# Head 0's inverse and its pool placed ahead of the closing of the projections' pools; the late gates through two buffers of their own

## The chip, the cores and the metric

The kernel runs on one core of one Trainium2 chip. TensorE (PE) multiplies and transposes, VectorE (DVE), ScalarE (ACT) and GpSimd (POOL) do the elementwise work, and SyncE (SP) issues every DMA from one queue, in order. PE writes its results to PSUM (eight banks); everything else lies in SBUF (224 KB for each of 128 partitions). The metric is the device time of one execution in microseconds; lower is better. All instructions of an engine run in the order in which they stand in its program, so an instruction that waits holds up what stands behind it.

## What is computed

One layer of an encoder trunk on 2048 tokens of width 1024: RMSNorm, one input projection, then two groups of heads, whose outputs meet in one output projection that is added to the residual. The parts that matter here:

```python
h = rms_norm(x, norm_w[l])
proj = h @ w_in[l]
(dn_q, dn_k, dn_v, dn_z, dn_beta, dn_decay,
 sw_q, sw_k, sw_v, sw_z) = jnp.split(proj, cuts, axis=-1)
dn = gated_deltanet_bidir(dn_q, dn_k, dn_v, dn_beta, dn_decay, ...)
dn = rms_norm(dn, dn_out_norm_w[l]).reshape(b, s, DN_WIDTH)
dn = dn * jax.nn.silu(dn_z)
sw = windowed_gqa_with_sinks(sw_q, sw_k, sw_v, ...)
sw = sw * jax.nn.silu(sw_z)
x = x + jnp.concatenate([dn, sw], axis=-1) @ w_out[l]
...
# in gated_delta_rule_chunked, for each head, direction and chunk:
m = jnp.where(strict, jnp.einsum('bhncd,bhnsd->bhncs', k_beta, k) * decay, 0.0)
t_inv = lax.linalg.triangular_solve(eye + m, eye, left_side=True, lower=True, unit_diagonal=True)
```

The DeltaNet group has four heads of width 128. Each head runs a recurrence over the sequence forward and backward, and each chunk of it needs the inverse of a triangular matrix.

## The kernel before

**Stages.** Phase A makes the normalised input, the projections with their gates and convolution, and the windowed attention; its results go to DRAM. Phase B runs the four DeltaNet heads one after another and then the output projection. For head `h`:

- `pre_front(h)` loads keys, queries and values in four groups of four chunks (order 1, 2, 0, 3), transposes them, makes the matrices `ma` and stores them to `m_d`. In each group a power of the keys' squared norms, `nk`, is taken on POOL (L684); `bp`, `ma` and the copy `vs` come after it.
- `solve(h)` loads the 32x32 diagonal blocks of all chunks (`X`, `L`) and inverts them column by column on DVE: 31 pairs of instructions (tiles `tm` and `X`), each pair waiting for the one before. It stores the result to `x_d`.
- `invert(h)` loads `x_d` back in pieces (`xc`), transposes them on DVE (`xt`), copies blocks into the tiles `iv` and `ma` on POOL, and makes the whole inverse with five groups of products on PE (tile `pi`) for each of four pieces (`hi` = 0 to 3).
- `scan(h)` runs 16 steps in both directions at once (tiles `pk`, `py`, `po` on PE; `r`, `S`, `oacc` on DVE; `yk`, `y` on ACT). Its first four steps need only piece 0 of the inverse. `post` normalises and gates the result.

`pre_front(h + 1)`, `solve(h + 1)` and `invert(h + 1)` stand behind `scan(h)` in the text and overlap it on the engines. The output projection's windowed half is cut into 32 units (`sw_units`, tile `pcs`), which fill PE in phase B. The other half (`out_dn`, tile `pcd`, weights `wohd`) ends the program.

**Late gates.** The gates of the second half of the sequence are left out of phase A and run between `pre_front(0)` and `solve(0)` as `late`: four calls of `gate_pairs`, eight output tiles `zo`, PE tile `pf_z`.

**Memory.** Tiles come from pools, which are laid on two stacks, one from each end of SBUF. A pool that opens where older pools lay has to wait for their work; `set_order` plans every use of its tiles behind the last use of all tiles of the older pools that it overlaps. At 128 partitions the places are, in bytes: `xp` 162656 to 228192 (input, split in two), `wp` 123488 to 162656 (weights), `bp` 102848 to 123488 (five buffers of 4128), all three on the right and in the stack `wide`, which is closed after `solve(0)`. On the left `hd0`, `q1` and `qa` (head 0's tiles, `pre_front`'s and `solve`'s) end at 87168. After the closing there open on the right `rp` (the scan's tiles; over `xp`), `hd1` (head 1's tiles; over `wp` and `xp`), `qb` 114912 to 147680 (the inverse's tiles, and two groups of head 2's keys and values; over `bp` and `wp`), and `swp` 88288 to 114912 (the windowed units; over `bp`). The pool `op` of the last projection opens at the end from 55936 to 109184, over `q1`, `qa` and `swp`.

**Order.** The text's order is not the order on the engines. `set_order` builds a graph of all instructions with edges for data, buffers, PSUM banks and pools, plans all engines over it several times with estimated durations, and pins each engine's queue to the best plan. So a change of a pool's place changes edges, and the plan with them, in the whole program.

Of the kernel before, what the change touches and what calls it, by code (L numbers as in the profile page):

```python
# [7 lines left out]
F32 = mybir.dt.float32  # L8
# [59 lines left out]
def phase_a(ctx, wide, tc, t, ident, nw, bd, gp, mix_sw, kq_d, v_d, zdn_d, zsw_d, q_pool):  # L68
# [5 lines left out]
    with tc.using_default_side("right"):  # L74
        xp = wide.enter_context(tc.tile_pool(reuse_waits="tile", name="xp", bufs=2))
        wp = wide.enter_context(tc.tile_pool(reuse_waits="tile", name="wp", bufs=2))
        bp = wide.enter_context(tc.tile_pool(reuse_waits="tile", name="bp", bufs=5))
        pj = wide.enter_context(tc.tile_pool(reuse_waits="tile", name="pj", bufs=3, space=PSUM))
# [127 lines left out]
    def gate_pairs(todo, half, mid=None):  # L206
        ws = [load_w(t["wt"][i // 2], 2 * P, f"z{i}_{half}") for i, _ in todo]
        for nb in range(2):
            for (i, dst), w in zip(todo, ws):
                o = bp.tile([P, 1030], F32, tag="big", name=f"zo{i}_{half}_{nb}")[:, :1024].rearrange("p (j s) -> p j s", j=2)  # L210
                for j in range(2):
                    ps = proj_feat(w, j * P, 2 * half + nb, f"z{i + j}_{half}_{nb}")
                    A.activation(o[:, j], ps, AF.Tanh, scale=0.5)
                    V.scalar_tensor_tensor(o[:, j], o[:, j], 1.0, ps, ALU.add, ALU.mult)
                at = half * 1024 + nb * 512
                for j in range(2):
                    dma(dst[j][:, at : at + 512], o[:, j])
# [169 lines left out]
    for half in range(2):  # L387
# [20 lines left out]
        sw = [lambda i=i: gate_pairs([(16 + i, [zsw_d[i], zsw_d[i + 1]])], half) for i in (0, 2)]  # L408
        conv = [lambda i=i: conv_pair(i, half) for i in (0, 4, 8, 2, 6, 10)]
        if half:  # L410
            fill = conv
            late = sw + [lambda i=i: gate_pairs([(12 + i, zdn_d[i : i + 2])], half) for i in (0, 2)]
# [108 lines left out]
def phase_b(ctx, wide, late, tc, t, ident, consts, hp, mix_dn, mix_sw, kq_d, v_d, zdn_d, zsw_d, dp, out):  # L521
# [97 lines left out]
    qa = pool("qa", stack=pre_stack)  # L619
    ps_i = [pool("ps_i0", stack=pre_stack, space=PSUM), pool("ps_i1", stack=pre_stack, space=PSUM)]  # L620
# [12 lines left out]
    def kv_tile(kind, h, n, name):  # L633
        p, slot = ((0, n), (1, n), (2, n) if n < 2 else (0, n - 2), (0, 2 + n) if n < 2 else (1, n - 2))[h]
        return (hd[p] if p < 2 else qb).tile([P, 4, P], F32, tag=f"{kind}{slot}", name=name, bufs=1)
# [659 lines left out]
```

## Time and profile before

| | us |
|---|---|
| median of three runs | 1291.93 (1291.03 to 1295.85) |
| the profiled execution | 1291.8 |
| its span, first to last instruction | 1290.0 |

| engine | busy, us | share of the span |
|---|---|---|
| PE | 1231.0 | 95% |
| DVE | 903.9 | 70% |
| ACT | 718.4 | 56% |
| POOL | 509.8 | 40% |

The profile's page lists busy time by engine and by groups of instructions; its views cut the same execution into windows, timelines and chains. Times are counted from the first instruction. A matmul's busy time holds its latency, so that matmuls that wait for each other look busier than they are; PE's work is better read from the step between the starts of matmuls that follow each other.

### The profile page before, as it was taken

Reading aid. Unit: us, or ns where it says so; the run is one execution under the profiler, and the core shown is the slowest. Engines: PE = TensorE matmul, PEld = TensorE weight load, DVE = VectorE, ACT = ScalarE, POOL = GpSimd, SP = SyncE. Lnnn points to the kernel's source line nnn. Section 1 sums busy time; section 2 is a strip of 40 time slices with the busy share of each in tenths; the row PEclk is TensorE's granted clock in tenths of the full one; section 3 lists DMA queues with packets and bytes.
Section 4 is the critical chain, followed back from the end, with each engine's and each line's share of the span. In section 5 each row is a group of like instructions: output and inputs, shape, how many; then the busy total and the mean of one; then the engine's idle time right before and its main releaser. Section 6 shows DMA issues by size and latency. Waiting matters only on the chain.

```text
span 1290.0 us, 22619 instructions
## 1 busy us (share of the span) xinstructions
PE 1231.0 (95%) x7162; PEld 1058.8 (82%) x7162; DVE 903.9 (70%) x2266; ACT 718.4 (56%) x2121; POOL 509.8 (40%) x876
## 2 busy tenths in 40 slices
PE   6999989999999999999999997999799899999998
PEld 6998778888889998888888886788688689898876
DVE  4422388999975689999986474689579869656433
ACT  5422254776744577777664325768657845675310
POOL 2230053757612297665320104833582482640000
PEclk9999999999999999999999997999999999999999
DMA  7442243322544433422127736966965875644765
GB/s 260 148 131 84 84 163 121 116 83 90 156 149 145 127 104 103 150 90 75 71 93 234 219 100 204 254 176 200 282 162 174 267 204 172 196 152 133 253 236 207
DMA packets 225511, 205.36 MB, mean 159 GB/s; under 512 B 48496, under 2 KB 175088, under 8 KB 225392
## 3 DMA queue, kind: packets, MB, share of 16 engines
q1 hardware_dynamic: 225392, 203.92, 50.9%
q8 instruction: 57, 0.93, 0.3%
q14 instruction: 62, 0.51, 0.1%
HBM read 138.79 MB, written 65.08 MB: 158 GB/s over the span
## 4 chain that ended last, share of the span: by engine, by line
PE 68%; DVE 13%; issue 6%; DMA 6%; ACT 4%; POOL 3%; SPq 0%; DVEq 0%; POOLq 0%; ACTq 0%
PE pf_c L190 5%; PE pf_c L191 5%; PE pf_c L192 5%; PE pf_z L190 4%; PE pf_z L191 4%; PE pf_z L192 4%; PE pi L772 3%; PE pt L364 3%; DVE acc L241 2%; PE pq_q L201 2%; PE pq_q L202 2%; PE pq_q L203 2%; PE pcd L563 2%; PE pcd L564 2%; PE pcd L562 2%
## 5 line engine op out<-in xcount | busy, mean ns | idle before, releaser
L190 PE MATMUL pf_c<-xhi,wh_c 128*128 128x512 f32 x384 | 151.2, 406 | 3.2 <-DVE acc L241 3.2
L241 DVE SCALAR_TENSOR_TENSOR acc<-pf_c,cw,acc 128x512 f32<-128x512 f32 (+2 forms) x192 | 140.0, 742 | 17.0 <-ACT acc L237 16.1
L191 PE MATMUL pf_c<-xlo,wh_c 128*128 128x512 f32 x384 | 151.0, 404 | 0.0
L192 PE MATMUL pf_c<-xhi,wl_c 128*128 128x512 f32 x384 | 149.8, 404 | 0.0
L359 POOL TENSOR_SCALAR pr<-pr,st 128x384 f32<-128x384 f32 (+1 forms) x128 | 84.8, 679 | 73.2 <-DVE st L357 49.9
L192 PE MATMUL pf_z<-xhi,wl_z 128*128 128x512 f32 x256 | 90.8, 401 | 0.0
L191 PE MATMUL pf_z<-xlo,wh_z 128*128 128x512 f32 x256 | 90.8, 399 | 0.0
L190 PE MATMUL pf_z<-xhi,wh_z 128*128 128x512 f32 x256 | 89.8, 400 | 0.0
L190 PEld LDWEIGHTS pf_c<-xhi,wh_c 128*128 128x128 f32 x384 | 72.7, 190 | 16.9 <-DVE acc L241 3.6
L350 ACT ACTIVATE pr<-pr,st 128x384 f32<-128x384 f32 (+1 forms) x128 | 76.1, 596 | 16.4 <-DVE st L349 14.3
L191 PEld LDWEIGHTS pf_c<-xlo,wh_c 128*128 128x128 f32 x384 | 72.6, 190 | 13.7
L192 PEld LDWEIGHTS pf_c<-xhi,wl_c 128*128 128x128 f32 x384 | 72.4, 189 | 13.8
L368 ACT ACTIVATE ph<-pt 128x512 fp32r<-128x512 f32 x92 | 53.7, 594 | 46.9 <-PE pt L364 41.3
L345 DVE CUSTOM_DVE_ANT_0 pr<-s,mask,sink 128x384 f32<-128x384 f32 (+1 forms) x128 | 72.7, 592 | 4.8 <-PE pt L364 2.5
L364 PE MATMUL pt<-ident,pr 128*128 128x128 f32 x368 | 71.5, 275 | 1.5 <-POOL pr L359 1.4
L826 ACT ACTIVATE yk<-py,ck 128x128 f32<-128x128 f32 x120 | 43.8, 365 | 48.4 <-PE py L821 47.2
L684 POOL TENSOR_TENSOR nk<-ssk,pw 128x4 f32<-128x4 f32 x16 | 16.9, 1059 | 131.0 <-DVE ssk L683 95.0
L703 DVE SCALAR_TENSOR_TENSOR ma<-gh,bp,dc 128x256 f32<-128x256 f32 x128 | 55.0, 476 | 19.4 <-PE gh L694 15.2
L369 DVE TENSOR_TENSOR pl<-pt,ph 128x512 fp32r<-128x512 f32 x92 | 62.0, 683 | 6.9 <-ACT ph L368 6.6
L364 PEld LDWEIGHTS pt<-ident,pr 128*128 128x128 f32 x368 | 48.1, 140 | 16.8 <-POOL pr L359 4.1
L202 PE MATMUL pq_q<-wh_q,xlo 128*128 128x256 f32 x256 | 61.5, 283 | 0.0
L201 PE MATMUL pq_q<-wh_q,xhi 128*128 128x256 f32 x256 | 61.1, 285 | 0.0
(253 smaller groups left out, 3798.4 us busy)
## 6 DMA issues: line engine op xcount, KB each, us to landing
kqc<-kq_d SPq DMA_DIRECT2D x120, 128.0 KB, 2.9
ws_c<-wt SPq DMA_DIRECT2D x48, 256.0 KB, 3.4
xr<-x SPq DMA_DIRECT2D x16, 512.0 KB, 5.3
ws_z<-wt SPq DMA_DIRECT2D x32, 256.0 KB, 3.6
kq<-kq_d SPq DMA_DIRECT2D x16, 512.0 KB, 5.4
m_d<-ma SPq DMA_DIRECT2D x32, 256.0 KB, 5.2
mxs<-mix_sw SPq DMA_DIRECT2D x32, 256.0 KB, 3.6
xrs<-x SPq DMA_DIRECT2D x32, 256.0 KB, 3.5
```

What stands on the lines that cost most here:

```text
L190: T.matmul(ps, hi[:, k, cs], xhi[b][:, k], start=(k == 0), stop=False)
L191: T.matmul(ps, hi[:, k, cs], xlo[b][:, k], start=False, stop=False)
L192: T.matmul(ps, lo[:, k, cs], xhi[b][:, k], start=False, stop=(k == KC - 1))
L201: T.matmul(ps[:, :n], xh, hi[:, k, :n], start=(k == 0), stop=False)
L202: T.matmul(ps[:, :n], xl, hi[:, k, :n], start=False, stop=False)
L241: V.scalar_tensor_tensor(av, ps[:, lo:], cw[:, i, k : k + 1], av, ALU.mult, ALU.add)
L345: V.tensor_tensor_reduce(pr[j][:, :n], ps[:, :n], mask[:, lo * P : hi * P], 1.0, sink[:, hh : hh + 1], ALU.add, ALU.max, accum_out=mx[:, j ...
L350: A.activation(pr[j][:, :n], pr[j][:, :n], AF.Exp, bias=nm[:, j : j + 1], accum_out=den[:, j : j + 1])
L359: G.tensor_scalar(pr[j][:, :n], pr[j][:, :n], den[:, j : j + 1], 1.0, ALU.mult, ALU.mult)
L364: T.transpose(pt[:, j], pr[j][:, (kb - lo) * P : (kb - lo + 1) * P], ident)
L369: V.tensor_tensor(pl, ptf, ph.bitcast(F32), ALU.subtract)
L703: V.scalar_tensor_tensor(ma[d, c4][:, c], gh[:, k], bp[:, d, cc : cc + 1], gms[d][:, c : c + 1].to_broadcast([P, 2, P]), ALU.mult, ALU.mult,)
```

## The change

`bp` is taken off the stack `wide` and closes with phase A. A new pool `qb` for the inverse opens beside `q1` and `qa` on the left, from 87168 to 111744: it lies over `bp` alone. The late gates write into a pool `zp` of two buffers, 115232 to 123488, also over `bp`. `solve(0)`, the six clearings of the `iv` tiles and `invert(0)` stand ahead of `wide.close()`. Head 2's keys and values, which lay in the old `qb`, get a pool `kx` (139488 to 147680, over `wp`), and `swp` moves to 112864 to 139488 (over `bp`, `zp` and `wp`). `op` stays in its place, which now is that of `q1`, `qa` and the new `qb`, and not of `swp`. The arithmetic is unchanged.

```diff
-        bp = wide.enter_context(tc.tile_pool(reuse_waits="tile", name="bp", bufs=5))
+        bp = ctx.enter_context(tc.tile_pool(reuse_waits="tile", name="bp", bufs=5))
...
-    def gate_pairs(todo, half, mid=None):
+    def gate_pairs(todo, half, mid=None, zp=bp):
...
-                o = bp.tile([P, 1030], F32, tag="big", name=f"zo{i}_{half}_{nb}")[:, :1024].rearrange("p (j s) -> p j s", j=2)
+                o = zp.tile([P, 1030], F32, tag="big", name=f"zo{i}_{half}_{nb}")[:, :1024].rearrange("p (j s) -> p j s", j=2)
...
-            late = sw + [lambda i=i: gate_pairs([(12 + i, zdn_d[i : i + 2])], half) for i in (0, 2)]
+            late = sw + [lambda zp, i=i: gate_pairs([(12 + i, zdn_d[i : i + 2])], half, None, zp) for i in (0, 2)]
...
     qa = pool("qa", stack=pre_stack)
+    qb = pool("qb", stack=pre_stack)
...
-        return (hd[p] if p < 2 else qb).tile([P, 4, P], F32, tag=f"{kind}{slot}", name=name, bufs=1)
+        return (hd[p] if p < 2 else kx).tile([P, 4, P], F32, tag=f"{kind}{slot}", name=name, bufs=1)
...
+    with tc.using_default_side("right"):
+        zp = pool("zp", 2, stack=wide)
     H = pre_front(0)
     for f in late:
-        f()
+        f(zp)
     solve(0, H)
+    zts = [[const(f"iv{j}_{i}", [P, 4, P], None, qb) for i in range(2 - j % 2)] for j in range(4)]
+    for grp in zts:
+        for a in grp:
+            G.memset(a, 0.0)
+    invert(0, H)
     wide.close()
     with tc.using_default_side("right"):
         rp = pool("rp", 2)
         hd.append(pool("hd1"))
         ps_s = pool("ps_s", space=PSUM)
-        qb = pool("qb", stack=pre_stack)
+        kx = pool("kx", stack=pre_stack)
         swp = pool("swp", SWW, stack=pre_stack)
-    zts = [[const(f"iv{j}_{i}", [P, 4, P], None, qb) for i in range(2 - j % 2)] for j in range(4)]
-    for grp in zts:
-        for a in grp:
-            G.memset(a, 0.0)
     fill = sw_units(swp)
-    invert(0, H)
```

(The two windowed gates in `sw` get the pool in the same way.) Since the plan decides the order, three places of it are shown. The line numbers of the change are one to three higher than those of before.

**PE, from the last matmul of the projections on.** `pf_z` is a late gate, `tr`, `gh` and `trv` belong to `pre_front(1)`, `pi` to `invert(0)`, `py` to `scan(0)`. Before:

```order
L192 MATMUL pf_z_1_1_8754<-xhi_4485,wl_z_1_8652 128x512
L674 MATMUL tr_1_0_9912<-ident,kq_1_9900 128x128 x4
L694 MATMUL gh_1_0_9944<-kq_1_9900 128x256 x2
L674 MATMUL tr_1_1_9927<-ident,kq_1_9900 128x128 x4
L711 MATMUL trv_1_9968<-ident,vt_1_9902 128x128 x4
L674 MATMUL tr_2_0_9988<-ident,kq_2_9978 128x128 x4
L694 MATMUL gh_1_1_9955<-kq_1_9900 128x256 x2
L674 MATMUL tr_2_1_10003<-ident,kq_2_9978 128x128 x4
L694 MATMUL gh_2_0_10020<-kq_2_9978 128x256
L711 MATMUL trv_2_10044<-ident,vt_2_9980 128x128 x4
```

The first `pi` stands four rows further on, behind the transposes of group 0, and the first `py` 17 rows behind that. With the change:

```order
L192 MATMUL pf_z_1_1_8761<-xhi_4485,wl_z_1_8659 128x512
L675 MATMUL tr_1_0_9919<-ident,kq_1_9907 128x128 x4
L773 MATMUL pi_0_0_8925<-iv_0_8891,g_0_8911 128x128 x4
L695 MATMUL gh_1_0_9951<-kq_1_9907 128x256
L675 MATMUL tr_1_1_9934<-ident,kq_1_9907 128x128 x4
L695 MATMUL gh_1_0_9951<-kq_1_9907 128x256
L773 MATMUL pi_0_0_8940<-b_0_8930,iv_0_8894 128x128 x4
L773 MATMUL pi_0_0_8947<-iv_0_8894,b_0_8930 128x128 x4
L712 MATMUL trv_1_9975<-ident,vt_1_9909 128x128 x4
L773 MATMUL pi_0_0_8956<-iv_0_8896,g_0_8911 128x128 x4
L675 MATMUL tr_2_0_9995<-ident,kq_2_9985 128x128 x4
```

The inverse moved ahead of `pre_front(1)`, and the first `py` stands 17 rows behind the last `pf_z` instead of 30.

**POOL, at the start of `pre_front(1)`** (`nk1` is its power, the other rows clear and fill the inverse's tiles). Before:

```order
L736 MEMSET X0_8784 128x32
L684 TENSOR_TENSOR nk1_9894<-ssk1_9893,pw_4992 128x4
L761 TENSOR_TENSOR g0_0_8923<-ma0_0_8125 128x512
L901 MEMSET iv0_0_8903 128x512
L901 MEMSET iv2_0_8906 128x512
L684 TENSOR_TENSOR nk1_9894<-ssk1_9893,pw_4992 128x4
```

With the change:

```order
L766 COPY iv2_1_8895<-xc0_1_2_8974 32x4x32
L766 COPY iv2_1_8895<-xt0_0_1_8971 32x4x32
L766 COPY iv2_1_8895<-xc0_1_2_8974 32x4x32
L766 COPY iv2_1_8895<-xt0_0_1_8971 32x4x32
L685 TENSOR_TENSOR nk1_9901<-ssk1_9900,pw_4992 128x4
L785 COPY ma0_0_8132<-xc0_1_3_8907 32x4x32
```

The first `nk1` stood first behind the clearing of `X0`; now 27 block copies of the inverse stand between the two, and all clearings of `iv` stand earlier.

**DVE, at the last columns of `solve(2)`** (`tm2`, `X2`), beside `scan(1)` (`r1`, `S1`, `oacc1`; the last number of `oacc1`'s source `po1` before the running one is the step). Before:

```order
L741 TENSOR_TENSOR tm2_30_12113<-L2_12016,X2_12017 128x31
L683 TENSOR_SCALAR ssk3_13095<-ssk3_13095 128x4
L849 SCALAR_TENSOR_TENSOR oacc1_0_10792<-po1_1_15_11437,egc_5026,oacc1_0_10792 128x128
L745 TENSOR_TENSOR X2_12017<-X2_12017,tm2_30_12113 128x31
L703 SCALAR_TENSOR_TENSOR ma3_0_13263<-gh3_0_1_13311,bp3_13097,dc3_0_0_13260 128x2x128
```

With the change:

```order
L742 TENSOR_TENSOR tm2_30_12120<-L2_12023,X2_12024 128x31
L851 TENSOR_TENSOR oacc1_3_10812<-po1_0_12_11263,oacc1_3_10812 128x128
L834 SCALAR_TENSOR_TENSOR S1_1_12_11291<-S1_1_11_11251,egt_5024,po1_1_12_11283 128x128
L746 TENSOR_TENSOR X2_12024<-X2_12024,tm2_30_12120 128x31
L686 RECIPROCAL ssk3_13102<-ssk3_13102 128x4
```

The solve of head 2 ended beside the last step of head 1's scan (15) and now ends beside step 12. For `solve(1)` the order goes the other way: its last three columns stood behind the last `r0` before, and the last seven do now; its first column stood behind `r0` of step 4 and now stands behind that of step 7.

At the end of the program two more things differ: on SP four of the eight loads of `wohd` stand ahead of the store of the last but one windowed unit, where all stood behind the last one's, and on PE the last windowed unit runs between steps 12 and 15 of `scan(3)` instead of beside step 12.

More of the change, by code (lines that the diff above doesn't have):

```diff
@@ L407, in phase_a @@
             consts = delta_setup(tc, t, ident, bd, gp, ap, bp, pj, q_pool)
-        sw = [lambda i=i: gate_pairs([(16 + i, [zsw_d[i], zsw_d[i + 1]])], half) for i in (0, 2)]
+        sw = [lambda zp=bp, i=i: gate_pairs([(16 + i, [zsw_d[i], zsw_d[i + 1]])], half, None, zp) for i in (0, 2)]
         conv = [lambda i=i: conv_pair(i, half) for i in (0, 4, 8, 2, 6, 10)]
```

## The prediction

> **What bounds the kernel now.** I read the page first, then windows, then the timelines where PE stands still. On the page, the row of PE, the 40 slices, and PE's clock:
>
> ```profile
> PE 1231.0 (95%) x7162; PEld 1058.8 (82%) x7162; DVE 903.9 (70%) x2266; ACT 718.4 (56%) x2121; POOL 509.8 (40%) x876
> PE   6999989999999999999999997999799899999998
> PEclk9999999999999999999999997999999999999999
> ```
>
> PE bounds the whole, and the worst slice after the start is the 25th, from 774 to 806 us. That is where the change works: the gates end, head 0's inverse and scan begin. The windows (PE and PEld busy, DVE, ACT, POOL, the granted clock, DMA):
>
> ```profile
> 783.00:817.00 34.00, 25.44 (x126) 19.74 (x124) 19.75 (x47) 24.08 (x106) 20.66 (x42) 0.75 0.90 256
> 850.00:912.00 62.00, 58.79 (x410) 52.56 (x410) 59.64 (x192) 46.22 (x196) 17.17 (x17) 1.00 0.63 192
> 912.00:935.00 23.00, 16.86 (x92) 13.80 (x92) 10.06 (x29) 11.27 (x42) 13.61 (x35) 0.93 0.97 290
> 1018.00:1043.00 25.00, 21.40 (x114) 17.66 (x115) 14.90 (x38) 15.51 (x59) 17.43 (x44) 0.93 0.86 248
> 1130.00:1195.00 65.00, 62.07 (x467) 57.08 (x467) 40.04 (x120) 42.32 (x147) 14.68 (x32) 1.00 0.46 144
> ```
>
> Two things are to be seen. From 783 to 817 PE is neither full nor at full clock. From 850 to 912 DVE is full (59.64 of 62): there `solve(1)` and `scan(0)` share it. At each change of heads PE waits again.
>
> The timelines of 777 to 817 give the chain:
>
> ```profile
> 777.50 0.32 SPq L746 DMA_DIRECT2D x_d<-X  x1
> 785.77 0.57 SPq L217 DMA_DIRECT2D zdn<-zo  x1
> 791.46 0.43 SPq L757 DMA_DIRECT2D xc<-x_d  x1
> 797.71 0.30 DVE L758 STREAM_TRANSPOSE xt<-xc 128x128 f32<-128x128 f32 x1
> 801.58 1.49 PE L772 MATMUL pi<-iv,g 128*128 128x128 f32 x6
> 816.48 0.49 PE L821 MATMUL py<-vs,ma 128*128 128x128 f32 x2
> ```
>
> The solve is stored at 777.5, but its first piece is fetched only at 791.5, behind the last store of a gate (785.8), whose tiles lie where the inverse's are to lie. The other heads show how long the same way takes without that wait, from the store of the solve to the first `py`:
>
> ```profile
> 911.26 0.55 SPq L746 DMA_DIRECT2D x_d<-X  x1
> 934.34 0.38 PE L821 MATMUL py<-vs,ma 128*128 128x128 f32 x2
> 1018.34 0.68 SPq L746 DMA_DIRECT2D x_d<-X  x1
> 1042.25 0.39 PE L821 MATMUL py<-vs,ma 128*128 128x128 f32 x2
> 1091.71 0.33 SPq L746 DMA_DIRECT2D x_d<-X  x1
> 1129.47 0.49 PE L821 MATMUL py<-vs,ma 128*128 128x128 f32 x2
> ```
>
> 23.1 us for head 1, 23.9 for head 2, 37.8 for head 3 (its scan 2 was still running), and 39.0 for head 0. Heads 1 and 2 are bound by their solves: the way from the store to `py` is the shortest seen, and scan `h` has ended.
>
> **The change part by part.** To sum, I measure what PE has to do. A pass of 128 columns takes 0.11 us and one of 512 takes 0.23 us:
>
> ```profile
> 1172.53 1.12 PE pi L772 x10
> 1210.80 0.91 PE pcd L563 x4
> ```
>
> (10 passes in 1.12, 4 in 0.91; the small fp32 products are two passes.) Counted so along PE's order of before, from the last gate matmul (783.6) to the first `py` of head 0 lies 15.5 us of work, on to head 1's first `py` 112 from the last gate matmul, then 91 to head 2's, 81 to head 3's, and 57 to the first `pcd` at 1194.9. The time beyond the work is therefore: stretch A (783.6 to 934.3) 150.7 - 112 = 38.7 us, B (to 1042.3) 107.9 - 91 = 17, C (to 1129.5) 87.2 - 81 = 6, D (to 1194.9) 65.4 - 57 = 8.5. Together 70 us; the change can only move these. In the changed order the same counts are 11, 115.5, 84, 79 and 62.
>
> *The inverse ahead of the closing (A).* The store of the solve stays at 777.5. Landings:
>
> ```profile
> x_d<-X SPq DMA_DIRECT2D x4, 512.0 KB, 4.4
> xc<-x_d SPq DMA_DIRECT2D x32, 64.0 KB, 4.2
> L763 POOL COPY iv<-xt 32x128 f32<-32x128 f32 x4 | 1.2, 289 | 0.3
> L684 POOL TENSOR_TENSOR nk<-ssk,pw 128x4 f32<-128x4 f32 x4 | 4.1, 1014 | 42.5 <-DVE ssk L683 42.4
> ```
>
> 777.5 + 4.4 = 782 for the fetch, which SP issues at once in the new order, + 4.2 = 786 to 787, + 1.5 for transpose and first copies: the first `pi` at 788 to 789 instead of 801.6. Of the chain behind it (14.9 us before, part of it at half clock) the shortest form is five products with an eviction each, some 9 us: `py` at 798. But `nk1` and the last `dc` mask of `pre_front(1)` ran on POOL before at
>
> ```profile
> 786.33 1.02 POOL L684 TENSOR_TENSOR nk<-ssk,pw 128x4 f32<-128x4 f32 x1 [35.37 <-DVE ssk L683]
> 820.10 1.27 POOL L665 TENSOR_TENSOR dc<-dc,dmask 128x512 f32<-128x512 f32 x1
> ```
>
> and in the new order 27 copies of 0.29 us, some 0.33 with their starts, stand ahead of `nk1`: it comes at 787 + 9 = 796. `vs` and `ma` of `pre_front(1)` wait for it, each transpose and `gh` of the next group waits for them through one PSUM bank, and PE's order has those ahead of the last products and of `py`. So `py` at 803 (798 to 809), 13 us earlier with 4.5 us less work done: 9 us won at this point.
>
> It isn't kept, I think. `hd1` still opens only with the closing, so `pre_front(1)` begins no earlier, and POOL makes it later. The last `dc` mask ended at 821.3. Now 76 copies (25 us), two sums `g` of 1.27, four `nk` of 1.01 and four masks of 1.27 stand between 787 and the last mask: 787 + 25 + 2.5 + 4 + 5 = 824 to 827. The blocks of head 1 then go out and come back some 4 us later, and the first column of `solve(1)`, at
>
> ```profile
> 849.86 0.20 DVE L741 TENSOR_TENSOR tm<-L,X 128x31 f32<-128x31 f32 x1
> ```
>
> now stands behind step 7 of the scan: 853 to 857. From there to its last column the order holds as much DVE work as before (the scan is three steps further, but all of `solve(1)` is still to do), and DVE was full: 61 us again, so x_d at 914 to 918 and head 1's `py` at 937 to 941. I take 940: 156.4 - 115.5 = 41, that is 2 us more than before. Bounds: if the solve starts where it did and all 9 us stay, 30; if POOL delays it by the full 9.7 us of `nk1`, 49.
>
> *Solve 2 earlier (B).* Before, its store at 1018.3 came when scan 1 had ended, and PE waited until 1042. In the new order its last column stands beside step 12 of the scan instead of step 15. By the durations of DVE's rows that is some 14 us of DVE work earlier, and the 24 us from store to `py` now overlap the scan's end. But `solve(2)`'s first column stands ahead of the first `r1`, and before its blocks were copied only 5 us behind that:
>
> ```profile
> 936.62 0.35 DVE L814 SCALAR_TENSOR_TENSOR r<-pk,negc,vs 128x128 f32<-128x128 f32 x1 [0.62 <-PE pk L812]
> 941.71 1.30 DVE L734 COPY L<-X 64x1024 f32<-64x1024 f32 x1
> ```
>
> So scan 1 may wait 3 to 5 us. I take 4 us less: 13. Bounds: 7 (all of the wait at 1018 to 1043 but the scan's last step) and 20.
>
> *Scan 2 to 3 (C).* The solve of head 3 ends before its scan in both; 5 us, between 3 and 9.
>
> *The end (D).* Before, the last weights waited for the last windowed unit, since `op` lay over `swp`:
>
> ```profile
> 1181.09 0.32 SPq L604 DMA_DIRECT2D part<-xrs  x1
> 1184.68 1.83 SPq L545 DMA_DIRECT2D wosd<-wout  x4
> 1194.89 0.71 PE L562 MATMUL pcd<-wohd,mhd 128*128 128x512 f32 x2
> ```
>
> Now `op` lies over the inverse's pool, half of the loads stand ahead of two stores, and the last unit (12 matmuls, 2.8 us) and parts of two more run inside the scan's last steps, where PE had nothing. I take 4 of 8.5, bounds 2 and 8.5.
>
> *Costs that I put at nothing.* The late gates through two buffers: each buffer is asked for again two tiles later, some 20 us of PE work, and a store lands in 3 us; the wait of the first gate for the convolution's last stores, issued at
>
> ```profile
> 690.46 1.79 SPq L250 DMA_DIRECT2D v_d<-acc  x2
> ```
>
> and landing some 4 us later, is covered by seven us of other ACT work ahead of it and by three PSUM banks. If that cover is gone, PE stops after 11 us of matmuls. The four transposes `xt` stand on DVE ahead of the last three gate results and hold them and their stores some 4 us; behind these stores on SP stand the fetches of the scan's later steps and of the windowed weights, needed 10 us later. Phase A keeps its order but for single rows; I take 0, between -3 and 3.
>
> **Sum:** 41 + 13 + 5 + 4.5 = 63.5 against 70: 6.5 us less, 1290.0 - 6.5 = 1283.5 of span. The profiled execution took 1291.8, 1.8 more than its span, and is 0.1 from the median. Predicted: 1285 us. Its own range, 1279 to 1290.
>
> **The clock** is a question of its own. In windows of 2 us:
>
> ```profile
> 786.00:788.00 2.00, 0.66 (x4) 0.42 (x4) 0.75 (x3) 1.19 (x10) 1.67 (x2) 1.00 0.77 268
> 790.00:792.00 2.00, 1.74 (x5) 1.29 (x5) 0.38 (x1) 1.75 (x9) 0.00 (x0) 0.50 0.89 203
> 802.00:804.00 2.00, 2.00 (x9) 1.81 (x8) 0.13 (x1) 2.00 (x10) 1.92 (x3) 0.50 1.00 285
> 806.00:808.00 2.00, 2.00 (x17) 2.00 (x18) 2.00 (x6) 1.99 (x7) 1.91 (x3) 1.00 0.83 238
> ```
>
> The clock fell to half some 3 us after PE ran dry and came back only after 802, when PE had been full for a few us. [...]
>
> **Rivals.**
>
> 1. *The 9 us stay.* POOL and DVE are less tight than I count, `solve(1)` starts at 846 and ends at 905. For it: from 784 to 850 DVE and POOL have room. Against it: 59.64 of 62. A 30, B 13, C 5, D 4.5: 52.5, 17.5 less: 1274. Chance 0.17.
> 2. *Nothing lasts.* All of A is given back and B's gain goes with scan 1's late start: A 41, B 17, C 6, D 6: 1292, within 1288 to 1296. For it: the bound of A and B is DVE's one chain of solves, and that isn't shorter. Chance 0.20.
> 3. *Slower: POOL's queue makes `pre_front(1)` late.* The place is `nk1`. If it runs at 796 and each group of head 1 follows 9 us later, `solve(1)` is stored at 921, A is 49, and the blocks of head 2, which `r1` now waits for, add 4 in B (21); C 6, D 6: 82, 12 more: 1304, and 1299 with D's gain. It decides from some 8 us of delay at the first column of `solve(1)`, that is from 858. For it: 27 copies in front. Against: before, POOL waited 42.4 us for `ssk` in this stretch, so the queue has slack later. Chance 0.17.
> 4. *The clock stays halved* until the scan is under way: 11 us of work take 22, `py` at 810, and nothing is won in A beyond that; 2 more there, since DVE bounds it: 1287. Chance 0.05.
> 5. *The change doesn't reach the inverse*, since the gates' first results wait for the stores behind `bp` and PE stops: 1292. Chance 0.03.
>
> **How the numbers follow.** My forecast has 0.38; the time is its own. A measurement of this kernel tells some 0.5% from no change, so faster means below 1285.5 and slower above 1298.4. Faster: half and a little more of the forecast (0.22), rival 1 (0.17), rests of the others 0.05: 0.44. Slower: rival 3 (0.16) and a rest of 0.02: 0.18. Same: 0.38. The range, 1273 to 1298, leaves out part of rivals 1 and 3.
>
> **What would show it.** Right: the first `xc` issued at 782 to 784, `pi` at 788 to 790, `py` of head 0 near 803; then the first column of `solve(1)` no earlier than 850 and head 1's `py` near 940; head 2's store of the solve ahead of scan 1's end, and its `py` at 1033 to 1039; `pcd` some 6 us earlier. Wrong: `solve(1)` before 848 (rival 1), after 858 (rival 3), `nk1` at 787 (my reading of POOL), or a difference that is there already before 690 us, in phase A, where I expect none.

## The result, and the profile after

The changed kernel takes 1292.88 us in the median of 12 runs (1288.8 to 1294.21), the kernel before 1293.44 in 12 (1291.03 to 1295.85). The ratio is 0.9986, with a 95% interval of 0.9976 to 0.9997: less than 2 us faster, where 7 were forecast (1285 against the 1291.93 then known). The time lies near that of the second rival ("nothing lasts", 1292), though only in part for that rival's reason. The profiles that follow show one execution of each kernel.

The page of the profiled execution (span 1291.1 us) has these rows for PE, its slices and its clock:

```profile
PE 1229.3 (95%) x7162; PEld 1057.3 (82%) x7162; DVE 896.4 (69%) x2266; ACT 715.8 (55%) x2121; POOL 509.4 (39%) x876
PE   6999989999999999999999999899689999999998
PEclk9999989999999999999998999999799999999999
```

The weak 25th slice (775 to 807 us) is full now. The weakest behind the start is the 29th (904 to 936), the change from head 0 to head 1, with a 6 where before had a 7. PE's clock no longer falls in the 25th slice, but in the 6th, the 22nd (678 to 710) and the 29th. The windows (PE, PEld, DVE, ACT, POOL, the granted clock, DMA share, GB/s) that the prediction showed of before:

```profile
783.00:817.00 34.00, 32.19 (x209) 28.11 (x208) 14.75 (x44) 23.58 (x102) 23.59 (x67) 1.00 0.70 197
850.00:912.00 62.00, 56.80 (x373) 49.36 (x372) 56.10 (x179) 42.98 (x186) 16.52 (x14) 1.00 0.77 219
912.00:935.00 23.00, 13.95 (x41) 9.88 (x40) 10.18 (x31) 8.38 (x34) 10.60 (x22) 0.70 0.91 280
1018.00:1043.00 25.00, 22.53 (x142) 19.19 (x143) 18.93 (x53) 20.64 (x87) 21.38 (x52) 1.00 0.83 236
1130.00:1195.00 65.00, 62.81 (x473) 58.34 (x472) 40.49 (x121) 41.39 (x142) 18.38 (x42) 1.00 0.59 177
```

From 783 to 817 PE is busy 32.2 of 34 us at full clock (25.4 at 0.75 before): the inverse does fill that hole. The timeline of the changed kernel at the same landmarks:

```profile
780.68 0.32 SPq L747 DMA_DIRECT2D x_d<-X  x1
784.25 0.37 SPq L758 DMA_DIRECT2D xc<-x_d  x1
794.04 0.39 PE L773 MATMUL pi<-iv,g 128*128 128x128 f32 x2
797.24 1.02 POOL L685 TENSOR_TENSOR nk<-ssk,pw 128x4 f32<-128x4 f32 x1 [1.82 <-DVE ssk L684]
805.44 0.39 PE L822 MATMUL py<-vs,ma 128*128 128x128 f32 x2
857.25 0.20 DVE L742 TENSOR_TENSOR tm<-L,X 128x31 f32<-128x31 f32 x1
916.56 0.32 SPq L747 DMA_DIRECT2D x_d<-X  x1
944.26 0.38 PE L822 MATMUL py<-vs,ma 128*128 128x128 f32 x2
1009.59 1.33 SPq L747 DMA_DIRECT2D x_d<-X  x1
1041.32 0.38 PE L822 MATMUL py<-vs,ma 128*128 128x128 f32 x2
1127.15 0.38 PE L822 MATMUL py<-vs,ma 128*128 128x128 f32 x1
1194.43 0.73 PE L562 MATMUL pcd<-wohd,mhd 128*128 128x512 f32 x2 [0.51 <-ACT mhd L554]
```

Head 0's `py` comes 11 us earlier, head 1's 10 us later, head 2's 1 us and head 3's 2 us earlier, and `pcd` 0.5 us earlier. One landmark that is not a head explains it: the last late gate ends at 793.8 us, where it ended at 783.6. From that end to the first `pcd` the changed kernel needs 400.7 us, the kernel before 411.3: 10.6 won. Ahead of it 10.2 are lost, and 1.6 behind the first `pcd`, in the last projection, whose cause is not shown. But for rounding that is the span's +1.1.

Of the 10.2, 2.1 are there already at 403 us (405.5 against 403.4), and up to there PE's order is the same in both; I put them down to the scatter of the start that is spoken of below. Where most of the rest goes is seen at the end of phase A. First five windows of the changed kernel, then two of the kernel before:

```profile
675.00:680.00 5.00, 4.98 (x26) 3.79 (x25) 4.33 (x10) 2.48 (x5) 2.09 (x4) 1.00 0.42 138
680.00:685.00 5.00, 5.00 (x24) 4.11 (x23) 1.99 (x5) 2.14 (x4) 0.00 (x0) 1.00 0.27 75
685.00:690.00 5.00, 2.00 (x9) 1.34 (x8) 5.00 (x9) 1.72 (x3) 0.00 (x0) 0.88 0.96 300
690.00:695.00 5.00, 5.00 (x14) 4.00 (x15) 4.66 (x7) 2.49 (x3) 0.00 (x0) 0.50 0.64 220
695.00:700.00 5.00, 5.00 (x24) 4.15 (x23) 3.34 (x8) 2.10 (x16) 2.42 (x4) 0.94 0.93 303
```

```profile
685.00:690.00 5.00, 5.00 (x27) 4.07 (x26) 4.99 (x8) 1.90 (x3) 0.00 (x0) 1.00 0.68 228
690.00:695.00 5.00, 5.00 (x27) 4.10 (x26) 3.62 (x9) 5.00 (x24) 1.02 (x1) 1.00 0.73 276
```

PE stands still for 3 us of 685 to 690 and then runs at half clock. In the changed kernel's timeline the last matmul of the convolution, the first late gate and DVE's work for the convolution are:

```profile
686.35 0.40 PE L192 MATMUL pf_c<-xhi,wl_c 128*128 128x512 f32 x1
689.75 0.80 PE L190 MATMUL pf_z<-xhi,wh_z 128*128 128x512 f32 x1 [3.00 <-DVE acc L241]
684.33 7.34 DVE L241 SCALAR_TENSOR_TENSOR acc<-pf_c,cw,acc 128x512 f32<-128x512 f32 x11 [1.45 <-ACT acc L237]
```

The three PSUM banks of the projections hold the last three groups of the convolution (24 matmuls each), and DVE takes four `acc` of 0.67 us for each. In PE's order of before, the last matmuls of these groups stand 31, 4 and 1 matmuls ahead of the first gate, and the first group's bank is free when PE comes to the gate. In the changed order they stand 15, 12 and 1 ahead: PE shared its time between the groups, all were finished within some 3.3 us, and DVE sat idle until 684.33. DVE's order then takes the first two groups in turns, so that the first group's bank came free only with the eighth `acc`, and the gate waited for that one (684.33 + 8 x 0.67 = 689.7). Taken one behind the other, the first group's four would by the same arithmetic have been done at 687.0, 0.3 us behind the last matmul of the convolution. So the order of DVE has a share in the stop beside that of PE; no run changes the one without the other.

For the stages I use two measures below. The **first gate** is the start of the first `pf_z` of the late gates. **Lost** is the time of PE beyond its work: for each matmul the step from its start to the next start, less what such a step takes in the quickest fifth of its kind in the kernel before. Positions of rows are counted in PE's order.

### The profile page after: what moved, and what is told of

It reads as the page before. It is cut to its first block, busy times and chain, and to the rows that moved or that the text cites. A ratio compares the mean times of both kernels' runs of the same rounds, so it can differ in the third digit from the quotient of the medians.

```text
span 1291.1 us, 22600 instructions
## 1 busy us (share of the span) xinstructions
PE 1229.3 (95%) x7162; PEld 1057.3 (82%) x7162; DVE 896.4 (69%) x2266; ACT 715.8 (55%) x2121; POOL 509.4 (39%) x876
## 4 chain that ended last, share of the span: by engine, by line
PE 66%; DVE 8%; ACT 7%; DMA 6%; POOL 6%; issue 6%; SPq 1%; POOLq 0%; DVEq 0%; ACTq 0%
PE pf_c L190 5%; PE pf_c L191 5%; PE pf_c L192 5%; PE pf_z L190 4%; PE pf_z L191 4%; PE pf_z L192 4%; PE pi L773 3%; PE pt L364 2%; DVE acc L241 2%; PE pq_q L201 2%; PE pq_q L202 2%; PE pq_q L203 2%; PE pcs L600 2%; PE pcd L562 2%; PE pcd L563 2%
## 5 line engine op out<-in xcount | busy, mean ns | idle before, releaser
L192 PE MATMUL pf_c<-xhi,wl_c 128*128 128x512 f32 x384 | 150.5, 404 | 0.0
L241 DVE SCALAR_TENSOR_TENSOR acc<-pf_c,cw,acc 128x512 f32<-128x512 f32 (+2 forms) x192 | 139.6, 741 | 14.1 <-ACT acc L237 13.1
L368 ACT ACTIVATE ph<-pt 128x512 fp32r<-128x512 f32 x92 | 53.8, 595 | 48.0 <-PE pt L364 39.6
L600 PE MATMUL pcs<-wohs,mhs 128*128 128x512 f32 x128 | 57.0, 445 | 6.5 <-ACT mhs L594 6.3
L565 DVE TENSOR_TENSOR xrd<-xrd,pcd 128x512 f32<-128x512 f32 x32 | 21.0, 684 | 57.8 <-PE pcd L564 57.8
```

The source lines that it names most:

```text
L192: T.matmul(ps, lo[:, k, cs], xhi[b][:, k], start=False, stop=(k == KC - 1))
L241: V.scalar_tensor_tensor(av, ps[:, lo:], cw[:, i, k : k + 1], av, ALU.mult, ALU.add)
L600: T.matmul(ps, mh[:, k], wh[:, k], start=(k == 0), stop=False)
```

## The experiments

Each ran beside the kernel before on the same chip. On the four chips used, the kernel before had medians of 1296.46, 1294.69, 1295.57 and 1294.36 us, so ratios are compared, not times. A ratio comes from all runs of a kernel, the stretches from the one that was profiled. The stretches in us; "last gate" is the start of the last `pf_z` matmul:

| kernel | ratio to before (95%) | first gate | lost, 400 us to last gate | last gate to head 1's `py` | on to head 3's | on to `pcd` | last gate to `pcd` |
|---|---|---|---|---|---|---|---|
| before | 1 | 682.4 | 39.1 | 151.1 | 195.1 | 65.4 | 411.7 |
| changed | 0.9986 (0.9976 to 0.9997) | 689.7 | 46.9 | 150.9 | 182.9 | 67.3 | 401.1 |
| e1 | 0.9955 (0.9936 to 0.9974) | 686.6 | 39.6 | 154.7 | 182.5 | 67.7 | 404.9 |
| e2 | 1.0096 (1.0076 to 1.0115) | 688.5 | 45.9 | 154.9 | 196.1 | 66.9 | 418.0 |
| e3 | 1.0031 (1.0013 to 1.0048) | 689.7 | 45.2 | 143.9 | 200.7 | 65.5 | 410.1 |
| e4 | 0.9890 (0.9870 to 0.9910) | 683.5 | 37.3 | 152.5 | 182.5 | 66.6 | 401.6 |
| e5 | 1.0024 (1.0009 to 1.0040) | 688.3 | 46.2 | 157.9 | 183.0 | 66.6 | 407.4 |
| e6 | 1.0064 (1.0045 to 1.0083) | 690.1 | 46.2 | 149.2 | 200.3 | 65.5 | 415.0 |
| e7 | 0.9946 (0.9929 to 0.9964) | 684.4 | 39.2 | 150.9 | 186.2 | 66.2 | 403.3 |
| e8 | 0.9990 (0.9973 to 1.0007) | 683.1 | 37.1 | 166.0 | 177.0 | 67.6 | 410.6 |
| e9 | 0.9945 (0.9928 to 0.9961) | 688.0 | 39.6 | 152.9 | 186.1 | 66.8 | 405.7 |
| e10 | 1.0108 (1.0080 to 1.0135) | 688.7 | 48.4 | 155.4 | 194.1 | 67.7 | 417.2 |
| e11 | 1.0021 (1.0008 to 1.0034) | 683.7 | 39.8 | 163.0 | 181.6 | 67.6 | 412.2 |
| e12 | 0.9933 (0.9916 to 0.9949) | 682.0 | 39.3 | 151.8 | 186.5 | 67.9 | 406.2 |

The start of the program scatters by itself: e1 has the order of before up to there, and its convolution began 3.7 us later (131.9 against 128.2). So absolute landmarks of the profiles carry some 3 us of that, and I read stretches.

**Phase A's order exchanged (e1, e2).** A table of instruction numbers, packed into a string, is read into the planner's constraints; it holds the order of phase A of the other kernel:

```diff
+    for row in zlib.decompress(base64.b64decode(ORDER_A)).decode().split(";"):
+        k, last = 0, None
+        for step in row.split(":")[1].split(","):
+            k += int(step)
+            if last is not None:
+                started[last].append(k)
+            last = k
```

> The changed kernel with phase A pinned, on every engine, to the order that it has in the kernel before (all instructions ahead of the loads of head 0; the rest is planned anew). Theory P: the changed kernel's phase A ends later because its own order is worse on the chip (first late gate at 689.8 instead of 682.4, PE standing still 3 us and then at half clock), and that hides a gain of some 10 us behind the gates. Then the first late gate is at 682 to 684, the last at 783 to 786, the first column of solve(1) at 848 to 852, head 1's first py at 933 to 938, and the time 1282 to 1286. Rival Q: the place of the gates is not what bounds it; solve(1) and the later solves take the time back, and the time is 1290 to 1294 although the gates end earlier. Rival R: with two buffers behind all of bp the first gates wait for the last stores of the convolution in this order too; PE stops for 3 to 6 us at about 695, and the time is 1288 to 1292.

> The kernel before with phase A pinned to the order of the changed kernel (its memory and the rest unchanged, planned anew). Theory P: the first late gate comes at 688 to 691, PE stands still for about 3 us ahead of it, the last gate ends at 791 to 794, everything behind it moves by the same amount, and the time is 1299 to 1304. Rival Q: the waits behind the gates take up the delay, and the time is 1291 to 1296.

With the order of before, the changed kernel has no stop, and its lost time in the table falls from 46.9 to 39.6; with the order of the change, the kernel before has the same stop, and 45.9. Windows from 685 to 695 of e1, and the first gate of e2:

```profile
685.00:690.00 5.00, 5.00 (x25) 4.10 (x24) 3.20 (x5) 2.30 (x4) 0.00 (x0) 1.00 0.97 331
690.00:695.00 5.00, 5.00 (x24) 4.12 (x23) 4.78 (x8) 2.73 (x6) 0.00 (x0) 1.00 0.52 163
```

```profile
688.45 0.72 PE L190 MATMUL pf_z<-xhi,wh_z 128*128 128x512 f32 x1 [3.00 <-DVE acc L241]
```

So it is the order, not the waiting for `bp`'s last stores: rival R falls, since e1 has that waiting too. The size was too hopeful: e1 is 0.3% under the changed kernel, some 4 us, and its landmarks come 2 to 5 us later than theory P had them (first gate 686.6, head 1's `py` 942.5). Its start was 3.7 us late, and the new plan needs 3.8 us more behind the gates. e2 is slower than expected, 6 of its 12 us coming from a poorer plan behind the gates (418.0).

**The pool of the late gates alone (e3).** The kernel before with `bp` closing with phase A and `zp` of two buffers, nothing else:

```diff
-        bp = wide.enter_context(tc.tile_pool(reuse_waits="tile", name="bp", bufs=5))
+        bp = ctx.enter_context(tc.tile_pool(reuse_waits="tile", name="bp", bufs=5))
...
+        zp = pool("zp", 2, stack=wide)
```

> The kernel before with one part of the change alone: the late gates write into a pool of two buffers that opens when bp has closed with phase A; the inverse and its pool stay where they were, behind the closing. Theory P, with the part named: it is this pool that changes the plan of phase A, so the late first gate, the still stand of about 3 us and the half clock are here too, nothing is won behind the gates, and the time is 1298 to 1304. If the order of phase A is only chance, that is not tied to this pool: first gate at 682 to 686 and 1291 to 1296.

```profile
689.74 0.80 PE L190 MATMUL pf_z<-xhi,wh_z 128*128 128x512 f32 x1 [3.01 <-DVE acc L241]
```

The stop is there, and little is won behind the gates in the sum (410.1 for 411.7). The time is 1.0031, 4 us slower, against 5 or more expected: that plan wins 7 us up to head 1's `py` and gives 6 back.

**Two of five buffers instead of a new pool (e4).** The changed kernel, but phase A takes its buffers in turn from three of `bp` and two of `zp`, which is open from the start; the places in memory stay. A late gate then waits for one buffer, not for all uses of `bp`:

```diff
-        bp = ctx.enter_context(tc.tile_pool(reuse_waits="tile", name="bp", bufs=5))
+        zp = wide.enter_context(tc.tile_pool(reuse_waits="tile", name="zp", bufs=2))
+        b3 = ctx.enter_context(tc.tile_pool(reuse_waits="tile", name="bp", bufs=3))
+        bp = Turns((b3, b3, b3, zp, zp))
```

> The changed kernel, but the two buffers of the late gates are two of bp's five (phase A takes turns through three of bp and two of a pool that stays open), so that the late gates wait for single buffers and not for all of bp. The inverse is where the change put it. Theory P: the first late gate is back at 682 to 685 without the 3 us wait, the last gate at 781 to 786, the gain behind the gates stays, and the time is 1281 to 1286. Rival Q: 1290 to 1294, with head 1's first py no earlier than 940. If any new plan of phase A costs time on the chip: 1288 to 1294 with other stand stills between 400 and 690 us.

As expected: 0.989, 14 us faster than before, the best of all. No stop, lost 37.3, and the 10 us behind the gates stay (401.6). The first gate follows the matmul ahead of it without a wait:

```profile
683.23 0.39 PE L203 MATMUL pf_c<-xhi,wl_c 128*128 128x512 f32 x1
683.46 0.40 PE L201 MATMUL pf_z<-xhi,wh_z 128*128 128x512 f32 x1
```

But this is not the changed kernel's phase A with a shorter wait: 3002 of PE's 3738 instructions ahead of the first gate stand at another place than before, from the start of the program on.

**Another plan of the same program (e5).** `if i == 10:` in place of the choice by the planner's estimate.

> The changed kernel with another of the plans that its own planner made (the eleventh of its twelve instead of the best by its estimate). If the bad end of phase A follows from the pool of the late gates (theory P, systematic): the first late gate is at 688 to 691 again, with PE standing still for 2 us or more just ahead of it, the last at 790 to 795, and the time within 0.4% of the kernel before. If it is the luck of one plan: first gate at 682 to 685, and 7 to 10 us (0.5% to 0.8%) faster than before.

```profile
688.30 0.80 PE L190 MATMUL pf_z<-xhi,wh_z 128*128 128x512 f32 x1 [3.01 <-DVE acc L241]
```

The same stop. With the changed kernel and e3 that is each of three plans with this pool and no rule added (e2 repeats the changed kernel's order); it isn't the luck of one. Why the planner comes to this order with this pool is not shown.

**Two of five buffers, without the inverse (e6).** e4's pools with the inverse and `qb` where they were before.

> The counterpart of the split version without the inverse: phase A takes turns through three buffers of bp and two of a pool that stays open, the late gates write into those two, and the inverse and its pool stay behind the closing as before. Theory P: phase A is no worse than before (first gate 682 to 686, lost time of PE ahead of the last gate as before or less), the first py of head 0 comes 40 us behind the last gate's start or less than before by nothing, and the time is within 4 us of the kernel before; then some 10 us of the split version's 14 are the inverse's and its pool's. Rival: the two buffers alone carry the gain, and this kernel is 10 us or more faster than before.

Not as expected: there is no stop, but lost time of 46.2 spread between 400 us and the last gate, the first gate is at 690.1, and the time is 8 us above that of the kernel before, where 4 was the bound. So turns by themselves don't make a good phase A. Behind the gates it needs 415.0, and e4 401.6: this pair has the inverse and its pools as its difference and shows 13 us for them there.

**What holds head 1 (e7, e8, e10, e11).** All four are e4 with one rule or cost more. e7: the loads of scan 0 not ahead of the load of `solve(1)`'s blocks.

```diff
+    solve1 = next(k for k in used[next(x for x in used if x.startswith("X1_"))] if insts[k][1] == "SP")
+    for x in used:
+        if x.startswith("kqc0_") and insts[used[x][0]][1] == "SP":
+            started[solve1].append(used[x][0])
```

> The split version with one more rule for the planner: the loads of scan(0)'s keys may not start ahead of the load of solve(1)'s blocks, so that scan(0) stays out of the way of pre_front(1), which it shares DVE, ACT and the DMA engines with. If the early scan is what holds solve(1) back: the first column of solve(1) comes 57 to 61 us behind the last gate's start (65.3 in the split version) and head 1's first py 5 us earlier, and the time is 3 to 6 us below the split version's. If pre_front(1) is bound by itself: the first column stays at 63 to 66 us behind the gate, and the time is the split version's or up to 4 us more.

The first column came 60.9 us behind the last gate, as the first theory says, but head 1's `py` only 1.7 us earlier, and head 2 and 3 gave back 3.7. The time is not 3 to 6 us below e4's but above it (0.9946 against 0.9890). An earlier start of `solve(1)` is worth little by itself.

e8 stores the matrices of `pre_front(1)` twice.

```diff
             for d in range(2):
+                if h == 1:
+                    dma(mm[d, s4, : P * P].rearrange("u (i j) -> i u j", j=P), ma[d, c4][:, :, 0])
```

> The split version with a cost doubled: each of the eight stores of pre_front(1)'s matrices (256 KB) is issued twice, once to a place that nobody reads, ahead of the real one. From 800 to 850 us the DMA engines of the split version were busy 77% to 100%. If the DMA engines bound pre_front(1) and so the start of solve(1), 2 MB more at some 280 GB/s put its first column 6 to 9 us later, head 1's first py by as much, and the whole by 4 to 8 us. If they don't, less than 2 us.

The windows from 800 to 850 of e4 and of e8, and the first column in each:

```profile
800.00:850.00 50.00, 44.34 (x284) 38.93 (x284) 32.55 (x83) 37.64 (x141) 25.89 (x42) 0.97 0.92 254
849.60 0.20 DVE L753 TENSOR_TENSOR tm<-L,X 128x31 f32<-128x31 f32 x1
```

```profile
800.00:850.00 50.00, 45.47 (x315) 41.06 (x316) 31.49 (x88) 40.04 (x147) 23.70 (x40) 1.00 1.01 282
858.75 0.20 DVE L757 TENSOR_TENSOR tm<-L,X 128x31 f32<-128x31 f32 x1
```

The DMA engines were 92% busy and became full; the column came 9.6 us later against the last gate (74.8 and 65.3), and the time rose by 1.0%, 13 us, where 4 to 8 were expected. That fits a bound by DMA, though the time rose by more than the column's delay, and the added stores change SP's queue and the plan as well.

e10 takes bytes away: for heads 1 to 3 only the diagonal blocks that the solve reads are stored.

```diff
-                dma(m_d[d, s4, : P * P].rearrange("u (i j) -> i u j", j=P), ma[d, c4][:, :, 0])
+                to = m_d[d, s4, : P * P].rearrange("u (i j) -> i u j", j=P)
+                for q in quads if h else [slice(0, P)]:
+                    b = q if h else slice(0, P)
+                    dma(to[q, :, b], ma[d, c4][q, :, 0, b])
```

> The split version with a suspected cost cut: of the matrices of heads 1 to 3 only the four diagonal blocks of 32x32 are stored, which are all that the solve loads (a quarter of the bytes, in pieces of 128 bytes instead of 512, with four DMAs for one). If the bytes bound pre_front(1): its first column comes 3 to 6 us earlier behind the last gate than the 65.3 us of the split version, and the time is 2 to 5 us below it. If the number of pieces bounds it, or SP's queue with 96 issues more: first column at 65 us or later, and the time the same or up to 6 us more.

The second way, and worse: 1.1% slower than before and 2.2% slower than e4, some 28 us, where up to 6 were expected. The stores of e4 from 790 to 850, then those of e10 (number, KB each, us to landing), and four of e10's issues on SP:

```profile
m_d<-ma SPq DMA_DIRECT2D x8, 256.0 KB, 6.1
```

```profile
m_d<-ma SPq DMA_DIRECT2D x32, 16.0 KB, 4.7
804.65 2.83 SPq L723 DMA_DIRECT2D m_d<-ma  x4
```

With a sixteenth of the bytes in a DMA the stores landed after 4.7 us for 6.1, and these four issues held SP's queue for 2.83 us. Phase A's plan is worse as well (lost 48.4), so the run does not separate bytes from issues: e8, with more bytes, took 13 us more than e4, but that fewer would win time is not shown.

e11 holds `solve(2)` back by 9 us against scan 1.

```diff
+    step = next(k for x in used if x.startswith("r1_0_3_") for k in used[x] if insts[k][1] == "DVE")
+    started[step].append(next(k for x in used if x.startswith("tm2_0_") for k in used[x]))
```

> The split version with solve(2) held back: its first column may not run ahead of r of step 3 of scan(1), which puts it some 12 us behind head 1's first py instead of 2.7 us, as in the kernel before (12.7 us). Theory B: the gain between the first py of head 1 and that of head 3 comes from solve(2), which can begin earlier against scan(1) when head 0's scan, and with it pre_front(2), begins earlier. Then head 2's first py comes 104 to 110 us behind head 1's (96.7 in the split version, 107.9 before), and the two stretches up to head 3's first py take 188 to 196 us together (182.5 and 195.1). If the gain has another source: 95 to 100 us and 180 to 186 us.

`solve(2)` began 11.3 us behind head 1's `py` as meant, but head 2's `py` came after 101.4 us and both stretches took 181.6: theory B, as I had put it, falls. The 10 us went all the same, ahead of head 1's `py` (163.0 for 152.5), where the rule does not reach directly: `solve(1)` began as in e4 but was stored 10.7 us later against the last gate (139.5 and 128.8). The planner had made another plan of the whole. So one rule can cost as much as the inverse wins, and which of its places the gain behind the gates comes from is not shown.

**The order of the last groups (e9, e12).** One rule for the planner in the changed kernel (e9) and in e4 (e12):

```diff
+    pe = lambda t: [k for x in used if x.startswith(t) for k in used[x] if insts[k][1] == "PE"]
+    started[pe("pf_c11_1_0_")[-1]].append(pe("pf_c11_1_1_")[0])
```

> The changed kernel with one rule more for the planner: the last group of the last convolution pair may not start on PE before the group that went into PSUM ahead of it has had its last matmul. In the changed kernel three groups end within 3.3 us, DVE needs some 2.8 us for each, and the first late gate waits for their banks. If that is the stop (theory P): no wait of 1 us or more of PE ahead of the first late gate, which starts at 682 to 685, the last one at 784 to 788, lost time of PE from 400 us to the last gate 39 to 42 us instead of 46.9, and the time 0.4% to 0.7% below the changed kernel's, that is a ratio to the kernel before of 0.991 to 0.995. If the stop only moves to another place: ratio 0.997 to 1.001.

> The split version together with the rule of the run before last, that the last convolution group on PE waits for the one ahead of it. In the split version no stop is left ahead of the first late gate, so the rule has nothing to take away there: the time should be the split version's, a ratio to the kernel before of 0.987 to 0.992, with differences of a few us that come from the new plan. If the rule by itself made the better plan: 0.985 or less.

e9 does what theory P says: no wait of PE, lost 39.6, and the ratio falls from 0.9986 to 0.9945, 5.3 us. The windows answer to those of the changed kernel above:

```profile
685.00:690.00 5.00, 5.00 (x23) 4.09 (x22) 2.00 (x4) 2.42 (x4) 0.00 (x0) 1.00 0.74 213
690.00:695.00 5.00, 5.00 (x26) 4.16 (x25) 5.00 (x9) 1.61 (x3) 0.00 (x0) 1.00 0.91 293
```

Only the gates did not come back to where they were expected: the first starts at 688.0 and the last at 789.1, since the program's start lost some 2 us more and its work stands in another order. With that and 4.6 us more behind the gates, the profiled execution of e9, the slowest of its six (1293.09 us; median 1288.4), doesn't show the gain in its span; the 5.3 us are read from the medians' ratio, and the lost time from the profile. In e4 the rule has no stop to remove. e12 is 0.4% slower than e4, a little outside the 0.987 to 0.992 expected, by a plan that needs 4.6 us more behind the gates; such is the scatter between plans.

## Why the prediction was wrong, step by step

- **The step that failed** is in the costs put at nothing: "Phase A keeps its order but for single rows; I take 0, between -3 and 3." It measured +10.2 up to the end of the last gate, which used up the 10.6 won behind it. Of PE's 3738 instructions ahead of the first gate, 1486 stand at another place than before; the two orders laid side by side say so, though not what it costs (in e4 3002 do, with less time lost). Of the 7.8 us of lost time that phase A has more after 400 us, 3.0 are the stop and some 2.5 the half clock (lost time from the first gate to the last, 6.1 against 3.6); for the other 2 no place is shown. e9, which removes both, loses 7.3 us less there and gains 5.3 us.
- The same part named three PSUM banks as cover for the first gate's wait. They covered it: e1 has the wait without a stop. What the banks did not cover was DVE's work when three groups end together. The rival about the gates (5) had the place right, at the stop of PE, but a wrong cause (the stores behind `bp`) and a wrong reach, since the inverse did gain. (Rival 3's second time, 1299, does not follow from its own sum: D's 6 are in the 82 already, and with the forecast's 4.5 it is 1302.)
- **The sum of waits behind the gates** was 63.5 by forecast, and by the same counts of work, from the end of the last gate on, it measured 60.1: A 150.5 - 115.5 = 35.0 (41 forecast), B 97.1 - 84 = 13.1 (13), C 85.8 - 79 = 6.8 (5), D 67.2 - 62 = 5.2 (4.5). So 10 us were won where 6.5 were forecast. By the pairs e3 and changed (9), e6 and e4 (13), before and e1 (7), it is the inverse's and its pools'. The plans scatter too, but the two kinds stay apart: the four kernels with the inverse behind the closing need 410.1 to 418.0 us from the last gate to `pcd`, and seven of the ten with it ahead 401.1 to 407.4. The other three add stores there (e8, e10) or hold a solve back (e11), and need 410.6 to 417.2.
- **A**, with the forecast in brackets: `py` of head 0 at 805.4 (803), the first column of `solve(1)` at 857.3 (853 to 857), its store at 916.6 (914 to 918), head 1's `py` at 944.3 (940). These hits are luck, for the whole stretch began 10 us late. Behind the end of the last gate the first column came after 63.5 us (66.3 before, 69 to 73 by forecast) and the store of `solve(1)` after 122.8 (127.7 before): earlier, not later. Head 1's `py` came as before against the last gate (150.9 and 151.1), so "it isn't kept" was right, but not for POOL's sake. The 27 copies took 9.2 us, as counted, but the forecast left the store of `solve(0)` 6.1 us ahead of the gates' end, and it came 13.1 ahead, so that the copies were over when `nk1` could run: it ran 3.4 us behind the end of the last gate (2.7 before), and its row names DVE's `ssk` as what it waited for, not the copies. The last 4.6 us of the gain went between the store of `solve(1)` and `py`, 27.7 us for 23.1, where PE was less busy than before and at a lower clock (912 to 935: 13.95 of 23 us at 0.70, and 16.86 at 0.93 before). POOL's order has a row of the windowed units ahead of the inverse's copies there:

```profile
927.85 1.26 POOL L591 TENSOR_TENSOR mxs<-mxs,zcs 128x512 f32<-128x512 f32 x1 [7.27 <-DMA zcs<-zsw_d]
929.05 0.61 POOL L764 COPY iv<-xc 32x128 f32<-32x128 f32 x2
```

What that wait is worth no run shows. Rival 3's mechanism falls with `nk1`, and rival 1 too: from the last gate to head 1's `py` nothing to speak of was won in any of the kernels with the inverse ahead. Of rival 2 the half on A came true; its half on B did not.
- **The first `pi`** came at 794.0 and not at 788 to 789. Its data were fetched from 784.25; in PE's order it stands behind the last gate, which ended at 793.8.
- **B**: `solve(2)` was stored ahead of scan 1's end as forecast, and the number fits. That its earlier place is the cause is not shown (e11). The wait of scan 1 for head 2's blocks that I feared didn't come: their load was issued at 936.27, ahead of head 1's `py` at 944.26.
- **D**: the loads of the last weights came at 1176.5 instead of 1184.7, and 5 us more of PE's work fitted into 2 us more of time.
- **The clock** (rival 4): 1.00 from 783 to 817, for 0.75 before. That it might stay halved was an estimate from the 0.50 that before shows from 790 to 804. PE was busy for 32.2 of these 34 us, the small products of the inverse among them. The clock was at half behind the stop in phase A instead (0.50 from 690 to 695).

## What to carry to other kernels

Where a planner sets the order, a change of a pool's place changes edges whose weight is passed back through the whole program: compare the orders stage by stage ahead of the change too, and take no stage for unchanged that has not been looked at. A pool opened over an old one waits for all of that one's users; a part of the same ring, kept open, waits for one buffer. The kernel with that (e4) was 12 us better than the changed one (0.9890 against 0.9986), but its phase A is another plan, and e6 and e10 with the same buffers lost as much time there as the kernels with the stop; so what the buffers are worth by themselves is not shown. Before groups that share few PSUM banks run interleaved on PE, count what the engine behind them needs when they end together (here DVE, with four `acc` of 0.67 us for each).

## What the runs showed of the hardware

A stop of PE of 3.0 us cost more than itself, in all four kernels that have it at the first late gate (changed, e2, e3, e5): 3.4 or 6.8 us at half clock came with it. Windows of 1 us, of the changed kernel and of e3 (PE's clock is the third number from the end):

```profile
688.00:689.00 1.00, 0.00 (x0) 0.00 (x0) 1.00 (x3) 0.27 (x1) 0.00 (x0) 0.89 0.99 318
689.00:690.00 1.00, 0.25 (x1) 0.26 (x2) 1.00 (x3) 0.00 (x0) 0.00 (x0) 0.50 1.02 352
695.00:696.00 1.00, 1.00 (x5) 0.80 (x4) 0.85 (x1) 1.00 (x8) 0.00 (x0) 0.70 0.73 142
```

```profile
689.00:690.00 1.00, 0.26 (x1) 0.26 (x2) 1.00 (x3) 0.00 (x0) 0.00 (x0) 0.88 1.05 293
693.00:694.00 1.00, 1.00 (x8) 0.81 (x7) 1.00 (x2) 0.10 (x1) 0.00 (x0) 0.91 0.50 164
```

In the windows of 1 us around these stops the clock is at 1.00 or at 0.50 but where it changes. I read a mean of 0.89 in one us as half clock for the last 0.22 of it, and so on; by that estimate it was at half from 688.8 to 695.6 in the changed kernel (6.8 us), from 689.8 to 693.2 in e3 (3.4 us), and for 3.4 us in e2 and e5. PE was at work again within 1 us of its beginning in all four; why it lasted twice as long in one of them is not shown. The length of a stop did not decide by itself whether the clock fell. The kernel before has one of 2.20 us at 1024.6, with 3.4 us of half clock from 1027.5 on, and e5 one of 3.37 us at 181.2, with the clock at 1.00 from 181 to 191:

```profile
1026.81 1.65 PE L878 MATMUL tro<-ident,oacc 128*128 128x128 f32 x5 [2.20 <-ACT oacc L875]
1028.00:1029.00 1.00, 1.00 (x4) 0.91 (x4) 1.00 (x3) 1.00 (x4) 0.09 (x1) 0.50 0.97 264
```

```profile
184.57 0.50 PE L190 MATMUL pf_c<-xhi,wh_c 128*128 128x512 f32 x1 [3.37 <-DVE acc L241]
181.00:191.00 10.00, 6.63 (x30) 5.26 (x29) 9.32 (x21) 5.24 (x13) 3.08 (x5) 1.00 0.11 33
```

What decides it is not shown; no run moves a stop to test it.
